# A two-layer decoder trunk on one core: the loads and squares at the start regrouped, and a new table of priorities for the order of all engines

## The chip, the cores and the metric

The kernel runs on one core of a Trainium2 chip. The metric is the time of one execution on the device, in microseconds (us); the figure for the kernel before is the median of three runs. The core has five engines that run side by side, each through its own row of instructions in a fixed order: TensorE (PE in the profile; PEld is its loading of stationary operands), VectorE (DVE), ScalarE (ACT), GpSimd (POOL) and SyncE (SP), which here only issues transfers. Sixteen DMA engines carry the transfers. An engine waits on semaphores for what another has to finish first.

## The reference

The input is x (256 tokens by 1024 features) and a condition c of 1024 values. Cut to its skeleton:

```
cs = silu(c)
for layer in range(2):
    sh1, sc1, g1, sh2, sc2, g2 = split(cs @ mod_w[layer] + mod_b[layer], 6)
    h = rms_norm(x, norm_g[layer, 0]) * (1 + sc1) + sh1
    if layer == 0:
        proj = h @ ab_w_in                       # 1024 -> 512 + 3 * 512
        y = concat(s5_mixer(proj[:512]), attention(proj[512:])) @ ab_w_out
    else:
        y = conformer_conv(h)    # GLU, causal conv of width 31, layer norm, silu, product
    x = x + g1 * y
    h = rms_norm(x, norm_g[layer, 1]) * (1 + sc2) + sh2
    x = x + g2 * conv_ffn(h)
return rms_norm(x, final_g)
```

What stands at the start of every layer, and what the change touches first, is this: the mean of the squares of x over its features, the modulation vectors from c, and then h, feature block by feature block, into the first product.

## The kernel before

Activations lie transposed: 128 features on the partitions, 256 tokens along the row, so x is eight tiles (kt = 0 to 7) of 128x256. Weights come from HBM in chunks of 512 KB (128x1024 f32). The names in the rows are buffers: `raw` and `ABT` hold weight chunks (raw_69 to raw_76 are eight of them, used over and over), `bank_61` to `bank_64` are the accumulators of the main products, `bank_65` to `bank_68` the auxiliary ones, `nt` (nt_98 to nt_101) the normalised feature tiles, `arena` the scratch space of the state-space part, `mrow` and `modv` the modulation vectors, `csv` the condition spread out as an operand, `hb` the conformer's normalised tile split in two parts for the product.

Nothing is issued as written. The functions record instructions, each with a group name (`nc.group`), and `flush` (L472), which is called after the first mixer, after the first FFN, after the conformer and at the end, hands each batch to `arrange` (L488). This is a list scheduler: it keeps a modelled clock for each engine and picks at each point the ready instruction of the highest rank. The rank is the longest path to the end plus a number from the table `BONUS` (L71) for the instruction's group. `cost` (L355) prices each instruction, a transfer by its bytes over a rate. At most eight transfers of SP and ACT are under way at once. Since every instruction is issued from one line of `flush`, all rows of the profile carry L485; the operands tell them apart.

At the start, `load` (L858) issues the small parameters (`pp`, whose first eight columns are c), x in two halves and the identity, clears a few buffers and derives `cs` and `csv`; `pump` (L602) streams weights. `start` (L1757) adds dummy products of a zero operand (groups `warm@t`, shown as `bank<-whi_81 128x512`) on PE, and the state-space preparation: `s5_poles` (66 small steps on DVE), `s5_powers` on POOL, then larger products on DVE (`arena` 128x256, 128x768 and 128x1024). `phase_a` (L1094) squares x, sums over the partitions on PE with a matrix of ones (`ones,nt`, `ones,u`), and from that makes the norm: DVE `nm`, ACT root, DVE `nm` again, DVE `dg`, and the PE product `dg,ones`, which spreads the factor over all partitions. For each kt it then runs `mods` (two halves of eight rows `raw,csv`), `select` (`sel,mrow`), `feature` (DVE `modv`, `gp`, `nt`, then ACT) and `main` (eight products `nt,raw` for kt below 4).

The conformer's layer norm, in the third batch, does the same in its middle: sums (`ones,nacc`, `ones,nt`, `negc,nt`), `nm`, `dg`, `dg,ones`, then DVE `nt`, ACT, DVE `hb`, and the next product `hb,whim`. Around it lie bundles of `raw,csv` and `ABT,csv` rows, the modulation of a later step, which need only their weights; in a bundle four chunks are used together, the rows of a chunk in a quarter of the array each.

Of the kernel before, what the change touches and what calls it, by code (L numbers as in the profile page):

```python
# [16 lines left out]
OP = mybir.AluOpType  # L17
# [262 lines left out]
class Plan:  # L280
# [74 lines left out]
    def cost(self, op):  # L355
        eng, fn, a, k, _ = op
        if fn == "dma_start":
            b = self.size(a[0]) * a[0].shape[0] * 4
            return max(0.06, b / 360e3)
# [187 lines left out]
class Emit:  # L547
# [298 lines left out]
    def modulate(self, l, j, q):  # L846
        nc = self.nc
        sh = self.modcols(l, 3 * j)
        self.h_u(0, q)
        for k in range(KT):  # L850
            if k + 1 < KT:
                self.h_u(k + 1, q)
            u, c = self.nt[k % 4], sh[:, k:k + 1]
            hi, lo = halves(self.h[:, k, :])
            nc.scalar.activation(hi, u, AF.Identity, bias=c)
            nc.vector.scalar_tensor_tensor(lo, u, c, hi.bitcast(F32), op0=OP.add, op1=OP.subtract)

    def load(self):  # L858
        nc, d = self.nc, self.d
        xv = d["x"].rearrange("(k p) t -> p k t", p=128)  # L860
        nc.sync.dma_start(self.pp[:, 0:NPAR_FIRST], d["pp"][:, 0:NPAR_FIRST])
        nc.sync.dma_start(self.x[:, 0:4], xv[:, 0:4])
        nc.sync.dma_start(self.x[:, 4:8], xv[:, 4:8])
        nc.sync.dma_start(self.ident, d["eye"][:, 0:128])
        nc.vector.memset(self.ones, 1.0 / D)
        nc.vector.memset(self.epst, EPS)
        nc.vector.memset(self.negc, -1.0 / 128)
        nc.vector.memset(self.zero2, 0.0)
        nc.sync.dma_start(self.sel, d["eye"][:, 256:260])
        nc.gpsimd.memset(self.csv, 0.0)  # L870
        nc.vector.memset(self.mrow[:, 0:512], 0.0)
        for t_ in self.AB + self.CA + [self.KD]:
            nc.gpsimd.memset(t_, 0.0)
        nc.vector.tensor_copy(self.zero, self.mrow[:, 0:512])
        self.warm(AF.Silu)
        nc.scalar.activation(self.cs, self.par("c", 0, 8), AF.Silu)
        self.warm(AF.Sqrt)
        for s in range(3):
            nc.vector.tensor_copy(self.csv[:, s, :, s], self.cs)
        nc.vector.tensor_scalar(self.gneg, self.par("norm", 0, 40), -512.0, None, op0=OP.mult)  # L880
# [213 lines left out]
    def phase_a(self):  # L1094
# [65 lines left out]
        for k in range(KT):  # L1160
# [4 lines left out]
            if k == 3:  # L1165
                v.tensor_tensor(sq[0], sq[0], sq[1], op=OP.add)
                v.tensor_tensor(sq[2], sq[2], sq[3], op=OP.add)
# [894 lines left out]
```

## Time and profile before

| | |
|---|---|
| three runs | 657.36, 657.41, 658.21 us; median 657.41 |
| profiled execution | 656.32 us |
| its span, first to last instruction | 654.5 us |
| PE busy | 641.0 us, 98% of the span |
| DVE, ACT, POOL busy | 548.3, 395.7, 52.8 us |
| mean granted clock of TensorE | 0.997 |

The profiled execution is 1.1 us below the median; 1.8 us of it lie outside the span. Its rows are read in the order of the kernel: what PE waits for, then the stretch in which a wait stands, engine by engine.

### The profile page before, as it was taken

The numbers are of one execution on the slowest core, as the hardware profiler recorded it, in microseconds if no ns is written. First come the engines' busy times: TensorE is split into PE (matmuls) and PEld (weight loads), VectorE is DVE, ScalarE is ACT, GpSimd is POOL, SyncE is SP. The second block draws the span as 40 slices with busy tenths as digits, with TensorE's granted clock in tenths as the row PEclk, the third lists the DMA queues.
The fourth block names the chain that finished last, engine by engine and source line by source line (L and its number), as shares of the span: only waits on it lengthen the run. The fifth ranks groups of instructions, "written<-read, shape, count | busy, mean of one in ns | idle before, by whom it ended". The sixth has DMA issues, their size and how long they took to land.

```text
span 654.5 us, 13232 instructions
## 1 busy us (share of the span) xinstructions
PE 641.0 (98%) x5125; PEld 564.0 (86%) x5125; DVE 548.3 (84%) x1097; ACT 395.7 (60%) x706; POOL 52.8 (8%) x101
## 2 busy tenths in 40 slices
PE   7999999999999999999999999999999999999995
PEld 6779956899999999998899987568988888888884
DVE  6899998578999999988867899569899999996642
ACT  4478444587866666654546843377596777774430
POOL 6690100000000000000000222000000000000000
PEclk9999999999999999999999999999999999999998
DMA  8996979456478899998862696595567777865001
GB/s 330 349 366 243 340 308 379 167 198 215 136 247 325 310 331 305 341 324 283 304 195 92 194 367 212 181 413 196 182 187 221 229 224 244 278 214 191 1 0 65
DMA packets 46566, 158.50 MB, mean 242 GB/s; under 512 B 5375, under 2 KB 9000, under 8 KB 46504
## 3 DMA queue, kind: packets, MB, share of 16 engines
q1 hardware_dynamic: 44936, 153.78, 67.2%
q0 software_dynamic: 1152, 3.49, 1.7%
q8 instruction: 40, 0.66, 0.4%
q10 hardware_dynamic: 416, 0.39, 0.2%
q14 instruction: 22, 0.18, 0.1%
HBM read 153.10 MB, written 1.06 MB: 236 GB/s over the span
## 4 chain that ended last, share of the span: by engine, by line
PE 94%; DVE 2%; ACT 2%; POOL 1%; issue 0%; DVEq 0%
PE bank L485 94%; POOL arena L485 1%; DVE nt L485 1%; ACT whim L485 0%; ACT h L485 0%; DVE x L485 0%; DVE whi L485 0%; ACT nt L485 0%; DVE arena L485 0%; ACT L485 0%; DVE h L485 0%; ACT cb L485 0%; DVE nm L485 0%; DVE g L485 0%; DVE mrow L485 0%
## 5 line engine op out<-in xcount | busy, mean ns | idle before, releaser
L485 PE MATMUL bank<-h,whi 128*128 128x256 f32 (+2 forms) x960 | 200.6, 303 | 0.0
L485 PEld LDWEIGHTS bank<-h,whi 128*128 128x128 f32 x960 | 151.3, 189 | 9.3 <-issue 1.8
L485 PE MATMUL bank<-h,wlo 128*128 128x256 f32 (+1 forms) x560 | 152.2, 282 | 0.0
L485 PE MATMUL bank<-h,whim 128*128 128x256 f32 (+1 forms) x664 | 150.0, 311 | 0.3 <-DVE h L485 0.3
L485 PE MATMUL bank<-h,wlom 128*128 128x256 f32 x416 | 116.6, 281 | 0.0
L485 PEld LDWEIGHTS bank<-h,whim 128*128 128x128 f32 x664 | 108.5, 189 | 8.4 <-DVE h L485 0.7
L485 PEld LDWEIGHTS bank<-h,wlo 128*128 128x128 f32 x560 | 103.2, 189 | 0.1
L485 DVE TENSOR_TENSOR wlo<-raw,whi 128x1024 fp32r<-128x1024 f32 x70 | 84.6, 1221 | 7.5 <-ACT whi L485 7.2
L485 ACT ACTIVATE whi<-raw 128x1024 fp32r<-128x1024 f32 x70 | 73.5, 1055 | 24.2 <-PE bank L485 12.0
L485 PEld LDWEIGHTS bank<-h,wlom 128*128 128x128 f32 x416 | 78.3, 188 | 0.0
L485 DVE TENSOR_TENSOR wlom<-raw,whim 128x1024 fp32r<-128x1024 f32 x57 | 69.3, 1221 | 7.4 <-ACT whim L485 7.3
L485 ACT ACTIVATE whim<-raw 128x1024 fp32r<-128x1024 f32 x57 | 59.7, 1054 | 23.5 <-PE bank L485 18.4
L485 PE MATMUL bank<-hv,whim 128*128 128x512 f32 (+1 forms) x236 | 67.7, 351 | 0.0
L485 PE MATMUL bank<-hv,whi 128*128 128x512 f32 x160 | 56.6, 394 | 0.0
L485 PE MATMUL bank<-hv,wlom 128*128 128x256 f32 x192 | 53.9, 281 | 0.0
L485 PEld LDWEIGHTS bank<-hv,whim 128*128 128x128 f32 x236 | 41.3, 188 | 6.2
L485 PE MATMUL bank<-hv,wlo 128*128 128x256 f32 x160 | 44.7, 279 | 0.0
L485 DVE SCALAR_TENSOR_TENSOR ac<-g,pp,ac 128x256 f32<-128x256 f32 x88 | 42.2, 482 | 2.2 <-ACT ac L485 0.4
L485 DVE SCALAR_TENSOR_TENSOR x<-bank,modv,x 128x256 f32<-128x256 f32 x54 | 25.6, 481 | 21.6 <-PE bank L485 20.7
L485 ACT ACTIVATE g<-bank 128x256 f32<-128x256 f32 x40 | 15.3, 382 | 39.2 <-PE bank L485 39.2
L485 PEld LDWEIGHTS bank<-hv,wlom 128*128 128x128 f32 x192 | 36.4, 189 | 0.0
L485 PEld LDWEIGHTS bank<-hv,whi 128*128 128x128 f32 x160 | 30.0, 187 | 7.1
(214 smaller groups left out, 1085.3 us busy)
## 6 DMA issues: line engine op xcount, KB each, us to landing
raw<-w_in SPq DMA_DIRECT2D x203, 512.0 KB, 5.2
ABT<-w_in SPq DMA_DIRECT2D x81, 512.0 KB, 5.0
a<-ap POOLq DMA_DIRECT2D x24, 142.0 KB, 5.6
x<-x_in SPq DMA_DIRECT2D x2, 512.0 KB, 4.6
arena<-scr SPq DMA_DIRECT2D x1, 1024.0 KB
cb<-c_in SPq DMA_DIRECT2D x2, 512.0 KB, 5.6
arena<-bc_in SPq DMA_DIRECT2D x1, 512.0 KB, 8.2
out<-x SPq DMA_DIRECT2D x2, 256.0 KB, 2.4
```

The lines of the kernel that those rows point to most:

```text
L485: getattr(getattr(self.nc, eng), fn)(*a, **k)
```

## The change

In `load`, c gets a transfer of its own (eight columns of `pp`) and goes first, on ScalarE's queue; the identity follows on the same queue. x goes in four transfers of 256 KB instead of two of 512 KB, on SP; `sel` and the rest of `pp` stay on SP. In `phase_a` the squares are taken in pairs of tiles (128x512), pairs 0 and 2 on ACT, 1 and 3 on DVE, into qT and u instead of nt and u; one addition for each pair follows on DVE, and still four sums go to PE. Each of these steps gets a group name of its own, so that the table can move it. There are 21 dummy products instead of 27. The model's transfer rate goes from 360e3 to 390e3 bytes per us. And every number of `BONUS` is new, so the order changes on all engines, most of all in the start and the first mixer.

```diff
-BONUS = {'a-evac': 702.8, 'a-gate_tail': -74.2, 'a-lead': 5, 'a-low': -1.7, ...
+BONUS = {'a-evac': 7.6, 'a-gate_tail': -3.3, 'a-h_u': -1.2, 'a-low': -0.6, ...
@@ def cost
-            return max(0.06, b / 360e3)
+            return max(0.06, b / 390e3)
@@ def load
-        nc.sync.dma_start(self.pp[:, 0:NPAR_FIRST], d["pp"][:, 0:NPAR_FIRST])
-        nc.sync.dma_start(self.x[:, 0:4], xv[:, 0:4])
-        nc.sync.dma_start(self.x[:, 4:8], xv[:, 4:8])
-        nc.sync.dma_start(self.ident, d["eye"][:, 0:128])
+        nc.group = "loadc"
+        nc.scalar.dma_start(self.pp[:, 0:8], d["pp"][:, 0:8])
+        for i in range(4):
+            nc.group = "loadx%d" % i
+            nc.sync.dma_start(self.x[:, 2 * i:2 * i + 2], xv[:, 2 * i:2 * i + 2])
+        nc.group = "loadid"
+        nc.scalar.dma_start(self.ident, d["eye"][:, 0:128])
+        nc.group = "loadsel"
+        nc.sync.dma_start(self.sel, d["eye"][:, 256:260])
+        nc.group = "loadpp"
+        nc.sync.dma_start(self.pp[:, 8:NPAR_FIRST], d["pp"][:, 8:NPAR_FIRST])
...
@@ def phase_a
-        sq = [t[:, 0:T] for t in self.nt] + [self.u[:, m].rearrange("p a b -> p (a b)") for m in range(4)]
-        for k in range(KT):
-            if k in (2, 6, 7):
-                v.tensor_tensor(sq[k], self.x[:, k, :], self.x[:, k, :], op=OP.mult)
-            else:
-                nc.scalar.activation(sq[k], self.x[:, k, :], AF.Square)
...
+        flat = self.u.rearrange("p a b c -> p a (b c)")
+        for i in range(4):
+            nc.group = "sq%d" % i
+            s, xs = (self.qT, flat)[i // 2][:, 2 * (i % 2):2 * (i % 2) + 2], self.x[:, 2 * i:2 * i + 2]
+            if i % 2:
+                v.tensor_tensor(s, xs, xs, op=OP.mult)
+            else:
+                nc.scalar.activation(s, xs, AF.Square)
+            v.tensor_tensor(s[:, 0], s[:, 0], s[:, 1], op=OP.add)
+            self.stat_mm(KT - 1 if i == 3 else 0, s[:, 0], st)
...
@@ def start
-        for i, t in enumerate([0.0] * 4 + [2.5 + WARM * i for i in range(int(11.5 / WARM))]):
+        for i, t in enumerate([0.0] * 4 + [2.5 + WARM * i for i in range(int(8.5 / WARM))]):
```

PE at the start, before, from the last of the seventeen opening dummies to the first `select` (`whi_81` rows are dummies, `ones,...` the sums of squares, `raw,csv` the modulation):

```order
L485 MATMUL bank_61<-whi_81 128x512
L485 MATMUL bank_68<-zero_109,ident 128x2
L485 MATMUL bank_68<-ones,nt_98 128x1 x2
L485 MATMUL bank_68<-ones,nt_100 128x1 x2
L485 MATMUL bank_68<-ones,u 128x1 x3
L485 MATMUL bank_65<-raw_69,csv 32x128 x8
L485 MATMUL bank_68<-ones,u 128x1
L485 MATMUL bank_65<-raw_70,csv 32x128 x8
L485 MATMUL bank_62<-whi_81 128x512
L485 MATMUL bank_63<-whi_81 128x512
L485 MATMUL bank_64<-whi_81 128x512
L485 MATMUL bank_68<-sel,mrow 128x2
```

And now, from the fifth dummy after `zero,ident` (twelve dummies stand before that row, four between) to the second half of `mods`:

```order
L485 MATMUL bank_61<-whi_81 128x512
L485 MATMUL bank_68<-ones,qT 128x1
L485 MATMUL bank_62<-whi_81 128x512
L485 MATMUL bank_68<-ones,qT 128x1 x3
L485 MATMUL bank_68<-ones,u 128x1 x2
L485 MATMUL bank_63<-whi_81 128x512
L485 MATMUL bank_64<-whi_81 128x512
L485 MATMUL bank_61<-whi_81 128x512
L485 MATMUL bank_65<-raw_69,csv 32x128 x8
L485 MATMUL bank_68<-ones,u 128x1 x2
L485 MATMUL bank_65<-raw_70,csv 32x128 x8
L485 MATMUL bank_66<-raw_71,csv 32x128 x8
```

The sums are spread out: three dummies and a half of `mods` stand ahead of the last two rows instead of the half alone ahead of the last one, and nine dummies that filled the row between `mods` and `main` are gone.

DVE at the features of kt = 2 (nt_100), before; the `arena` rows are the state-space products, 128x16x16 and 128x256 the first six, 128x16x48 the next:

```order
L485 TENSOR_TENSOR arena<-arena 128x16x16 x2
L485 TENSOR_TENSOR arena<-arena 128x256
L485 TENSOR_TENSOR arena<-arena 128x16x16 x2
L485 TENSOR_TENSOR arena<-arena 128x256
L485 TENSOR_TENSOR arena<-arena 128x16x48
L485 TENSOR_TENSOR modv_88<-bank_68,pp 128x1 x2
L485 SCALAR_TENSOR_TENSOR gp<-modv_88,gneg 128x1
L485 SCALAR_TENSOR_TENSOR nt_100<-x,gp,bank_67 128x256
```

And now:

```order
L485 TENSOR_TENSOR arena<-arena 128x16x16 x2
L485 TENSOR_TENSOR modv_88<-bank_68,pp 128x1
L485 TENSOR_TENSOR arena<-arena 128x256
L485 SCALAR_TENSOR_TENSOR gp<-modv_88,gneg 128x1
L485 TENSOR_TENSOR arena<-arena 128x16x16 x2
L485 SCALAR_TENSOR_TENSOR nt_100<-x,gp,bank_67 128x256
L485 TENSOR_TENSOR arena<-arena 128x256
L485 TENSOR_TENSOR modv_88<-bank_68,pp 128x1
L485 TENSOR_TENSOR arena<-arena 128x16x48 x2
```

The feature of kt = 2 moves ahead of the sixth small product and of the first large one.

PE in the conformer's layer norm, before, from the product that spreads the norm to the first products with `hb`:

```order
L485 MATMUL bank_65<-dg,ones 128x256
L485 MATMUL bank_64<-ABT_86,csv 32x512 x2
L485 MATMUL bank_64<-raw_73,csv 32x512
L485 MATMUL bank_64<-ABT_85,csv 32x512
L485 MATMUL bank_66<-zero_109,ident 128x2
L485 MATMUL bank_61<-hb,whim_1644 128x512
L485 MATMUL bank_61<-hb,wlom_1645 128x256
L485 MATMUL bank_62<-hb,whim_1646 128x512
L485 MATMUL bank_62<-hb,wlom_1647 128x256
L485 MATMUL bank_63<-hb,whi_79 128x512
L485 MATMUL bank_67<-raw_69,csv 32x512
L485 MATMUL bank_67<-ABT_85,csv 32x512
```

And now:

```order
L485 MATMUL bank_65<-dg,ones 128x256
L485 MATMUL bank_67<-raw_69,csv 32x512
L485 MATMUL bank_67<-ABT_85,csv 32x512
L485 MATMUL bank_67<-raw_76,csv 32x512
L485 MATMUL bank_67<-raw_72,csv 32x512
L485 MATMUL bank_64<-raw_69,csv 32x512
L485 MATMUL bank_64<-ABT_85,csv 32x512
L485 MATMUL bank_64<-raw_76,csv 32x512
L485 MATMUL bank_64<-raw_72,csv 32x512
L485 MATMUL bank_61<-hb,whim_1637 128x512
L485 MATMUL bank_61<-hb,wlom_1638 128x256
```

The two bundles of raw_69, ABT_85, raw_76 and raw_72 stood behind the first five `hb` rows and now stand ahead of them; the bundle with ABT_86 that stood there has moved ahead of `dg,ones`. The product `sg,ones`, which stood between the first two bundles of the same four buffers further up, has moved behind four of these bundles. On SP the loads that fill the four buffers anew come in the same order in both kernels, those after the change being:

```order
L485 DMA raw_69<-w_in 128x1024
L485 DMA ABT_85<-w_in 128x1024
L485 DMA raw_76<-w_in 128x1024
L485 DMA raw_72<-w_in 128x1024
L485 DMA raw_74<-w_in 128x1024
```

## Rows read from the trace of the kernel before

**Rows 1.** The page's first part: busy us, share of the span, instructions
```profile
PE 641.0 (98%) x5125; PEld 564.0 (86%) x5125; DVE 548.3 (84%) x1097; ACT 395.7 (60%) x706; POOL 52.8 (8%) x101
```

**Rows 2.** Waits of PE over the whole span: us in total, times, longest
```profile
PE bank L485 <- DVE dg L485: 1.7, 1, 1.7
PE bank L485 <- DVE hb L485: 0.8, 1, 0.8
PE bank L485 <- DVE modv L485: 0.7, 1, 0.7
```

**Rows 3.** Timeline of PE, 0 to 15 us: start, us, operation, count of records
```profile
3.55 6.52 PE L485 MATMUL bank<-whi 128*128 128x512 f32 x17 [3.55 <-DVE whi L485]
...
10.15 1.03 PE L485 MATMUL bank<-ones,nt 128*128 128x1 f32 x8
...
12.36 0.38 PE L485 MATMUL bank<-ones,u 128*128 128x1 f32 x2
12.67 0.64 PE L485 MATMUL bank<-raw,csv 128*32 128x128 f32 x16
13.24 0.97 PE L485 MATMUL bank<-whi 128*128 128x512 f32 x3
```

**Rows 4.** Stretches: PE, PEld, DVE, ACT, POOL busy (count), PEclk, DMA share, GB/s
```profile
3.55:8.60 5.05, 5.05 (x12) 3.98 (x13) 1.22 (x6) 1.03 (x3) 5.05 (x3) 1.00 0.99 344
...
10.00:20.00 10.00, 10.00 (x110) 8.34 (x110) 9.55 (x79) 5.77 (x15) 1.32 (x1) 1.00 1.03 406
...
25.40:29.00 3.60, 2.64 (x31) 2.12 (x27) 3.08 (x11) 2.19 (x7) 3.05 (x11) 1.00 0.93 345
...
40.00:50.00 10.00, 10.00 (x110) 8.34 (x109) 9.96 (x14) 7.64 (x13) 7.98 (x12) 1.00 0.96 342
```

**Rows 5.** Timeline of DVE, 9 to 28 us
```profile
9.69 0.76 DVE L485 TENSOR_TENSOR u<-x 128x256 f32<-128x256 f32 x2 [2.32 <-DMA x<-x_in]
...
12.78 0.16 DVE L485 TENSOR_SCALAR nm<-bank 128x2 f32<-128x2 f32 x1
...
15.73 0.48 DVE L485 SCALAR_TENSOR_TENSOR nt<-x,gp,bank 128x256 f32<-128x256 f32 x1
...
23.62 2.53 DVE L485 TENSOR_TENSOR arena<-arena 128x256 f32<-128x256 f32 x6 [1.91 <-POOL arena L485]
...
27.88 0.48 DVE L485 SCALAR_TENSOR_TENSOR nt<-x,gp,bank 128x256 f32<-128x256 f32 x1
```

**Rows 6.** Timeline of PE, 17 to 29 us: from `main` of kt = 0 to kt = 2
```profile
17.44 1.13 PE L485 MATMUL bank<-nt,raw 128*128 128x256 f32 x4
...
18.55 5.00 PE L485 MATMUL bank<-nt,raw 128*128 128x256 f32 x22
...
28.95 1.35 PE L485 MATMUL bank<-nt,raw 128*128 128x256 f32 x5 [0.28 <-ACT nt L485]
```

**Rows 7.** Timeline of PE in the conformer's layer norm
```profile
420.88 0.70 PE L485 MATMUL bank<-sg,ones 128*128 128x256 f32 x2
...
426.65 0.70 PE L485 MATMUL bank<-dg,ones 128*128 128x256 f32 x2
...
429.43 0.50 PE L485 MATMUL bank<-hb,whim 128*128 128x512 f32 x1 [0.77 <-DVE hb L485]
...
430.55 0.62 PE L485 MATMUL bank<-raw,csv 128*32 128x512 f32 x1
...
432.78 0.39 PE L485 MATMUL bank<-hb,wlo 128*128 128x256 f32 x1
```

**Rows 8.** Timeline of PE's weight loads, the bundle behind `hb`
```profile
430.95 0.17 PEld L485 LDWEIGHTS bank<-raw,csv 128*32 128x32 f32 x3 [0.25 <-DMA raw<-w_in]
```

**Rows 9.** SP's issues to the four buffers: timeline, then time from issue to landing
```profile
422.59 0.33 SPq L485 DMA_DIRECT2D raw<-w_in  x1
...
424.59 0.38 SPq L485 DMA_DIRECT2D raw<-w_in  x1
...
raw<-w_in SPq DMA_DIRECT2D x1, 512.0 KB, 6.3
```

More of the change, by code (lines that the diff above doesn't have):

```diff
@@ L860, in load @@
         xv = d["x"].rearrange("(k p) t -> p k t", p=128)
-        nc.sync.dma_start(self.pp[:, 0:NPAR_FIRST], d["pp"][:, 0:NPAR_FIRST])
-        nc.sync.dma_start(self.x[:, 0:4], xv[:, 0:4])
-        nc.sync.dma_start(self.x[:, 4:8], xv[:, 4:8])
-        nc.sync.dma_start(self.ident, d["eye"][:, 0:128])
+        nc.group = "loadc"
[9 more added lines that the diff above has]
+        nc.sync.dma_start(self.pp[:, 8:NPAR_FIRST], d["pp"][:, 8:NPAR_FIRST])
+        nc.group = "set"
         nc.vector.memset(self.ones, 1.0 / D)
@@ L868, in load @@
         nc.vector.memset(self.zero2, 0.0)
-        nc.sync.dma_start(self.sel, d["eye"][:, 256:260])
         nc.gpsimd.memset(self.csv, 0.0)
         nc.vector.memset(self.mrow[:, 0:512], 0.0)
-        for t_ in self.AB + self.CA + [self.KD]:
+        for i, t_ in enumerate(self.AB + self.CA + [self.KD]):
+            nc.group = "clear%d" % i
             nc.gpsimd.memset(t_, 0.0)
+        nc.group = "zero"
         nc.vector.tensor_copy(self.zero, self.mrow[:, 0:512])
+        nc.group = "cond"
         self.warm(AF.Silu)
@@ L878, in load @@
         for s in range(3):
+            nc.group = "cond%d" % s
             nc.vector.tensor_copy(self.csv[:, s, :, s], self.cs)
+        nc.group = "gneg"
         nc.vector.tensor_scalar(self.gneg, self.par("norm", 0, 40), -512.0, None, op0=OP.mult)
@@ L1760, in start @@
         self.pump(5)
+        nc.group = "loadbc"
         nc.sync.dma_start(self.BC, self.d["bc"].rearrange("p (a b c) -> p a b c", a=4, b=16))
         self.pump()
+        nc.group = "loadpp2"
         nc.sync.dma_start(self.pp[:, NPAR_FIRST:], self.d["pp"][:, NPAR_FIRST:])
+        nc.group = "loadanti"
         nc.sync.dma_start(self.anti, self.d["eye"][:, 128:256])
-        for i, t in enumerate([0.0] * 4 + [2.5 + WARM * i for i in range(int(11.5 / WARM))]):
+        for i, t in enumerate([0.0] * 4 + [2.5 + WARM * i for i in range(int(8.5 / WARM))]):
             nc.group = f"warm@{t:.2f}"
```

11 lines of the change are left out of this document (1 added, 10 removed).

## Prediction

> **What bounds the kernel now.** I read the page first: PE is busy for 641.0 of 654.5 us [rows 1], so the time is PE's row of instructions plus its few holes. The list of PE's waits [rows 2] names them: 1.7 us in the final norm, 0.8 in the conformer's layer norm (for `hb`) and 0.7 at the third feature tile (for `modv`); every other wait after the start is 0.3 or less. The first mixer, where the order changes most, has none. So a new order there can save nothing in itself; it can only hand on what the start saves, or add waits. Gains can come from three places: the start up to `main` of kt = 2, the layer norm's hole, and the final norm, whose order is the same before and after. The profiled execution took 656.32 us, 1.09 below the median of 657.41; I work out a difference and subtract it from the median.
>
> **The start.** PE runs dummies from 3.55, twelve of them in 5.05 us [rows 3, 4], 0.42 each; the three at 13.24 take 0.97, 0.32 each. [...] The sums of squares end with the row at 12.36, so that `mods` follows at 12.67 and DVE's `nm` at 12.78 [rows 3, 5].
>
> After the change I add PE's row up by durations. Twelve dummies end at 8.6. Then come the identity product (two records; eight of the similar sums take 1.03, so 0.26), five dummies (1.6), one sum row (0.26), one dummy (0.32), five sum rows (1.3), three dummies (0.97), half of `mods` (0.64) and two sum rows (0.52): 14.5. These are busy times, which overlap by about 0.07 at each change (`mods` at 12.67 takes 0.64 and the next row starts at 13.24); with some eight changes the end is 13.8 to 14.5. I take 14.0, 1.3 later than 12.67.
>
> Does x come in time for that? The second half lands at 9.68 [rows 5]. The order shows 2.10 MB on SP up to and with it; after the change 2.72 MB stand up to and with the last quarter. The extra 0.62 MB take 1.5 us at the 406 GB/s of 10 to 20 us or 1.8 at the 344 of the opening [rows 4]: 11.2 to 11.5; scaling the whole way from the first issue gives 12.2. A square of a pair (two tiles, 0.76 [rows 5]) and an addition (half that) bring the last sum to 12.4 to 13.4, before PE is there at about 13.5. So x in quarters costs nothing and gains nothing, and what hides it is the dummies and `mods`; c and the identity, earlier or not, are hidden by the twelve dummies.
>
> From `nm` to the first `nt` DVE takes 2.95 us [rows 5]; four small steps fewer stand between now, some 0.2 less. That gives `nt` at 12.78 + 1.3 + 2.75 = 16.8. From an `nt` to its `main` the third tile shows 1.07 (27.88 to 28.95 [rows 5, 6]), so `main` of kt = 0 starts at 17.9 instead of 17.44, where half a us of `mods` stood in between.
>
> From there to `main` of kt = 2 PE needs 11.51 us before, of which 0.7 and 0.28 are waits [rows 2, 6]: 10.5 of work. Of this work half a `mods` (0.64) and one `select` (0.25) now lie ahead of `main`, hidden in the hole of the norm chain; two more changes between kinds of rows cost 0.2. That leaves 9.8, and `main` of kt = 2 is reached at 27.7, if its operand is there. On DVE the third `nt` waits for five small products instead of six small and one large one. They begin when POOL releases them, at 23.62 before [rows 5]; DVE's small steps end a little later now, as the norm comes 1.3 later but ten of them (0.16 for a step as short as `nm` [rows 5], less where they overlap) were moved ahead of it, so I take 24.1. Five products of 0.42 and 0.3 for `modv` and `gp` give `nt` at 26.5, and `main` 1.07 later, 27.6. Both arms meet at 27.7, against 28.95: 1.2 gained. Since PE's row in this stretch must run without any hole for that, I take **0.9**, with 0 (PE's end at 14.5, a late x) and 1.4 as ends.
>
> **The layer norm.** At first sight two bundles now fill the 0.77 us in which PE waits for `hb`. But the four buffers of these bundles are being loaded anew. Before the change the bundle starts at 430.55, behind the first `hb` rows, and the weight load of its fourth buffer still waits 0.25 us, until 430.95, for a transfer [rows 7, 8]. That is raw_72, fourth of the four issues that begin at 422.59; it is issued at 424.59 and lands 6.3 later, at 430.9 [rows 9]. The loads can start once the first bundles have read the buffers, and these come earlier only by `sg,ones`, which takes at most 0.70 [rows 7] and has moved behind them. So raw_72 lands at 430.2 to 430.9, and PE, which gets to this bundle a little after `dg,ones` and therefore about 428.5, must wait there some 1.7 us, with the ready `hb` queued behind it. Before, all of this work (two bundles, five `hb` rows) is done at 432.78. After: 430.2 + 1.85 for the bundles (430.95 to 432.78) + 1.12 for the `hb` rows (429.43 to 430.55 [rows 7]) = 433.2 to 433.9. **Loss 0.4 to 1.1; I take 0.5**, since SP's order of the four loads is the same and nothing else holds them up. If the third load doesn't lag as it does here, where over a us passes before the fourth issue follows, raw_72 could land up to a us sooner, and 0.2 to 0.5 would be gained instead: that is the other end, a gain of 0.9 only if the wait vanished wholly.
>
> **The rest.** The mixer's PE work is the same in another order: I set it at 0, between 0 and 2. DVE is busy for 9.96 of 10 us at 40 to 50 [rows 4], so little can be caught up there. Fewer dummies save nothing by themselves, since those removed lay in holes of the norm chain. The sum: -0.9 + 0.5 = -0.4, profiled 655.9, median **657.0**.
>
> **Rivals.** *Both places gain* (faster). The start gives its 0.9 and the loads of the layer norm land in time, so that its hole of 0.8 to 0.9 goes as well: -1.8, 655.6; with 1.4 at the start, 655.1. For it: the bundles would be just the work that PE lacks there. Against it: the landing at 430.9, which would have to come at about 428.5.
>
> *The mixer takes it back* (slower). The place is DVE from 30 to 110 us: its state-space products start 0.5 later (24.1 for 23.62) while PE wants its tiles 0.9 earlier. DVE has no idle time to make that up [rows 4], so PE waits until it is back in step with DVE: 0.5 late instead of 0.9 early. With 0.5 to 1.1 from the layer norm that is +1.0 to +1.6, 658.4 to 659.0; I price it at 659.0. It decides from the point where POOL's release comes after 24. Against it: DVE is idle 1.91 us just ahead of that release [rows 5], and a large product can be put off where a feature cannot.
>
> [...]
>
> *It does not do what it says.* The squares come no sooner in PE's row, so the start stays where it was and only the layer norm's loss is left: 657.9, inside the first case's own range.
>
> **How the numbers follow.** A difference of 0.2%, 1.3 us, is about what a measurement of this kernel can tell from none. The forecast, 657.0 with its own range of 656.2 to 658.5 and the last rival in it, gets 0.46. Both places gain: 0.27, and with it all gains I have not seen. The mixer takes it back: 0.18. The clock falls: 0.09. So faster 0.27, within 0.2% 0.46, slower 0.27. The range leaves out a tenth at either side: 655.2 to 659.5.
>
> **What would show it.** The last sum row should end near 14.0 and `nm` follow; `main` of kt = 2 should start at 27.6 to 28.3 with no wait for `modv`; the state-space products on DVE should start near 24.1; the layer norm should have a wait of 1 to 2 us for a transfer in the bundle right behind `dg,ones` and none for `hb`; the list of PE's waits should hold nothing above 0.5 in the mixer; the granted clock should be 1.00 at `main` of kt = 0. I am wrong if raw_72 lands before 429, if the mixer shows waits for DVE, or if the dummies' durations show a slow stretch after 13.

## The result and the profile after

The changed kernel takes 662.96 us (median of 6 runs, 661.43 to 664.17) against 657.38 (6 runs, 656.58 to 659.21) for the kernel before: ratio 1.0081, interval [1.0067, 1.0096]. It is 5.6 us slower, where 657.0 and at most 659.5 were predicted. The profiled execution took 664.17, the slowest of the six; its span is 662.3, 7.8 more than that of before. On the chip that ran e5 to e8 below, the kernel before itself took 656.5 to 658.2 us in 6 of 25 runs and 662.9 to 666.3 in the other 19.

The page's first part (busy us, share, instructions) answers to [rows 1], and the list of PE's waits to [rows 2]:

```profile
PE 646.0 (98%) x5119; PEld 566.5 (86%) x5119; DVE 549.4 (83%) x1096; ACT 393.1 (59%) x703; POOL 48.5 (7%) x101
```

```profile
PE bank L485 <- DVE qT L485: 3.7, 1, 3.7
PE bank L485 <- DVE whi L485: 2.9, 1, 2.9
PE bank L485 <- DVE dg L485: 1.7, 1, 1.7
PE bank L485 <- DVE arena L485: 0.8, 1, 0.8
```

PE is busy 5 us longer, with six instructions fewer: the same work ran slower. And there is one large new wait, for qT, the squares of x's second pair; a small one, 0.8 us for `arena`, lies in the mixer. The wait for `whi` is the start of the first dummies, 3.55 us before and 2.87 now. The timeline of PE shows where it lies, for comparison with [rows 3] and [rows 6]:

```profile
9.15 0.28 PE L485 MATMUL bank<-ones,qT 128*128 128x1 f32 x2
13.10 1.01 PE L485 MATMUL bank<-ones,qT 128*128 128x1 f32 x4 [3.67 <-DVE qT L485]
13.97 0.99 PE L485 MATMUL bank<-ones,u 128*128 128x1 f32 x4
14.82 1.63 PE L485 MATMUL bank<-whi 128*128 128x512 f32 x3
...
17.39 1.01 PE L485 MATMUL bank<-ones,u 128*128 128x1 f32 x4
...
23.86 5.14 PE L485 MATMUL bank<-nt,raw 128*128 128x256 f32 x16
```

From 9.43 to 13.10 PE has nothing to do. Behind that hole the three dummies take 1.63 us instead of 0.97 [rows 3], and each row of four sums about 1.0 us, where e16 below has 0.50 to 0.61. The stretches (PE, PEld, DVE, ACT, POOL busy, PEclk, DMA share, GB/s) say why:

```profile
8.00:13.00 5.00, 1.43 (x9) 1.16 (x7) 4.60 (x12) 0.00 (x0) 3.45 (x2) 1.00 1.03 406
13.20:23.80 10.60, 10.60 (x101) 8.28 (x101) 5.91 (x44) 1.33 (x5) 0.00 (x0) 0.50 0.92 326
...
27.00:40.00 13.00, 13.00 (x138) 10.01 (x140) 10.04 (x24) 6.59 (x13) 11.90 (x34) 1.00 0.78 272
```

The granted clock is at half, 0.50, from 13.2 on, and back up at 1.00 from 27; before the change it is 1.00 here throughout [rows 4]. `main` of kt = 0 starts at 23.86 instead of 17.44.

Why did qT come so late? x did not: the second pair had landed at 9.11, the fourth at 11.11. DVE's timeline shows what stood in front:

```profile
8.36 0.90 DVE L485 COPY arena<-pp 128x16 f32<-128x16 f32 x1 [0.45 <-DMA pp<-pp_in]
8.44 0.84 DVE L485 TENSOR_SCALAR gneg<-pp 128x40 f32<-128x40 f32 x1
9.29 2.19 DVE L485 TENSOR_SCALAR arena<-arena 128x16 f32<-128x16 f32 x1
9.37 2.11 DVE L485 TENSOR_TENSOR arena<-pp 128x16 f32<-128x16 f32 x1
11.52 0.17 DVE L485 TENSOR_SCALAR arena<-arena 128x16 f32<-128x16 f32 x1
...
11.90 0.69 DVE L485 TENSOR_TENSOR qT<-x 128x512 f32<-128x512 f32 x1
12.50 0.17 DVE L485 SCALAR_TENSOR_TENSOR arena<-arena 128x16 f32<-128x16 f32 x1
12.62 0.42 DVE L485 TENSOR_TENSOR qT<-qT 128x256 f32<-128x256 f32 x1
```

Eight small steps stand ahead of the square `qT<-x`, seven of the state-space part and `gneg`. The first waits for its parameters, and two of them last 0.90 and 2.19 us where the same kind of step takes 0.17 at 11.52; the steps queued right behind these two, at 8.44 and 9.37, end with them. POOL's timeline has the reason: they end as its clears end, at 9.23 and 11.45.

```profile
7.42 1.81 POOL L485 MEMSET KD<- 128x2048 f32 x1
9.16 2.29 POOL L485 MEMSET CA<- 128x2560 f32 x1
```

In the kernel before these steps stood behind all squares and met the last clear only at its end.

The layer norm of the conformer answers to [rows 7] and [rows 8], PE first, then its weight loads:

```profile
436.33 1.04 PE L485 MATMUL bank<-raw,csv 128*32 128x512 f32 x2 [0.29 <-DMA raw<-w_in]
437.62 0.62 PE L485 MATMUL bank<-raw,csv 128*32 128x512 f32 x2 [0.24 <-DMA raw<-w_in]
...
439.45 0.50 PE L485 MATMUL bank<-hb,whim 128*128 128x512 f32 x1
```

```profile
436.33 0.14 PEld L485 LDWEIGHTS bank<-raw,csv 128*32 128x32 f32 x2 [1.19 <-DMA raw<-w_in]
437.62 0.11 PEld L485 LDWEIGHTS bank<-raw,csv 128*32 128x32 f32 x2 [1.15 <-DMA raw<-w_in]
```

The weight loads of two bundles wait 2.3 us for transfers (PE itself stands still for 0.5 of them), and `hb` is queued behind them.

Counted between rows that stand equally far from the last product (only `main` of kt = 0 stands 18 rows nearer to it now), the 7.8 us of the two profiled executions split so: +6.42 up to `main` of kt = 0, +0.04 in the first mixer, -0.01 from there to the conformer, +0.30 and +0.66 in the conformer's two halves, +0.09 behind it, and +0.32 between the last product and the end.

### The profile page after: what moved, and what is told of

It reads as the page before. It is cut to its first block, busy times and chain, and to the rows that moved or that the text cites. A ratio compares the mean times of both kernels' runs of the same rounds, so it can differ in the third digit from the quotient of the medians.

```text
span 662.3 us, 13210 instructions
## 1 busy us (share of the span) xinstructions
PE 646.0 (98%) x5119; PEld 566.5 (86%) x5119; DVE 549.4 (83%) x1096; ACT 393.1 (59%) x703; POOL 48.5 (7%) x101
## 3 DMA queue, kind: packets, MB, share of 16 engines
HBM read 153.10 MB, written 1.06 MB: 233 GB/s over the span
## 4 chain that ended last, share of the span: by engine, by line
PE 92%; DVE 4%; DMA 3%; SPq 0%; issue 0%; ACT 0%; DVEq 0%; ACTq 0%
PE bank L485 92%; DVE arena L485 2%; DMA raw<-w_in 1%; DMA ABT<-w_in 1%; DMA pp<-pp_in 1%; SPq L485 0%; DVE wlo L485 0%; DVE x L485 0%; DVE U L485 0%; ACT whi L485 0%; DVE qT L485 0%; DVE KD L485 0%; DVE nm L485 0%; DVE dg L485 0%; DVEq L2035 0%
## 5 line engine op out<-in xcount | busy, mean ns | idle before, releaser
L485 ACT ACTIVATE whim<-raw 128x1024 fp32r<-128x1024 f32 x57 | 59.7, 1053 | 24.5 <-PE bank L485 17.5
L485 DVE SCALAR_TENSOR_TENSOR x<-bank,modv,x 128x256 f32<-128x256 f32 x54 | 25.5, 481 | 21.5 <-PE bank L485 20.8
L485 ACT ACTIVATE whi<-ABT 128x1024 fp32r<-128x1024 f32 x27 | 28.2, 1054 | 14.6 <-DMA ABT<-w_in 8.6
L485 DVE TENSOR_TENSOR wlo<-ABT,whi 128x1024 fp32r<-128x1024 f32 x27 | 33.5, 1248 | 4.1 <-ACT whi L485 4.0
```

Of the source, the lines that this page charges most:

```text
L485: getattr(getattr(self.nc, eng), fn)(*a, **k)
```

## The experiments

All ratios are against runs of the kernel before on the same chip. The text calls a run by the first part of its name, e1 to e18, and PE's wait for qT the hole.

**The clock and the hole.** Sixteen more dummies in the hole:

```diff
+            if i == fill:                      # ahead of the second pair's sum
+                for _ in range(FILL_HOLE):     # 16
+                    <dummy product>
```

> The changed kernel with 16 more dummy products (some 0.23 us each) in PE's row just ahead of the sum of the second pair of squares, where PE idles for 3.67 us (9.43 to 13.10). The sum itself comes no sooner. Theory 'the idle hole drops the clock and the lower clock does the damage': PE stays busy, the granted clock stays at 1.00 from 10 to 30 us (0.66 in the changed kernel), main of kt = 0 starts near 19.2 instead of 23.86, and the time falls by 4 to 5 us, to about 658.5. Rival 'the late square alone, or the mixer's new order, does the damage': the same start of main within 1 us and no change of the time (663.0).

658.83 us, 1.0032 [1.0017, 1.0047] (before: 656.84). The late square is untouched, but the clock stays up:

```profile
13.20:19.70 6.50, 6.26 (x102) 4.69 (x101) 5.77 (x43) 1.30 (x4) 0.00 (x0) 1.00 1.04 405
```

```profile
19.78 3.72 PE L491 MATMUL bank<-nt,raw 128*128 128x256 f32 x16 [0.23 <-ACT nt L491]
```

`main` of kt = 0 starts at 19.78, 4.1 earlier than in the changed kernel and 2.3 later than before. So of the 6.4 us at the start of the changed kernel's profiled execution 4.1 are the clock and 2.3 the late square itself. What PE does from there to the end of the mixer takes 124.70 us for 126.99 before: the new order is 2.3 shorter there. About 0.9 of that are rows that now stand ahead of `main` of kt = 0 (half a `mods` and one `select`); 1.2 of the 2.3 fall ahead of `main` of kt = 2, 1.1 behind it.

**The order on DVE.** The second pair's square and addition ahead of the small steps:

```diff
+        late = [i for i in order if ops[i][4] == "sq1" and ops[i][0] == "vector"]
...
+            order = order[:at] + late + [i for i in order[at:] if i not in late]
```

> The changed kernel with one move on DVE: the square and the addition of the second pair of x stand ahead of the small state-space steps instead of behind the eighth of them. Theory 'these small steps, held first by the parameters' transfer (landed 8.34) and then by POOL's clears, hold the square up while x has been there since 9.11': the addition ends near 10.2 instead of 13.0, PE's hole shrinks from 3.7 to about 0.8 us, the clock stays at 1.00, main of kt = 0 starts at 17.5 to 18.5, and the time falls by 5 to 6 us, to 657 to 658. Rival 'the transfer of x is what is late': the hole stays above 3 us.

659.6 us, 1.0042 [1.0025, 1.0059]: half of the loss is left. The square now starts as x lands, and takes its 0.69 us beside a clear:

```profile
8.67 0.69 DVE L489 TENSOR_TENSOR qT<-x 128x512 f32<-128x512 f32 x1 [1.46 <-DMA x<-x_in]
```

The wait for qT is gone, but now the steps are in the way of the fourth pair, and PE waits 1.5 us for u; the clock still falls in the profiled execution (the 48 records of `raw,csv` at 14.74 take 2.32 us, for 1.52 in e1). `main` of kt = 0 starts at 19.76, not at 17.5 to 18.5: I had not asked where the stretched steps would go.

**The clears.** Two of POOL's five clears (CA and KD) on ACT, the order on DVE untouched:

```diff
+        late = [i for i in order if ops[i][4] in ("clear2", "clear4")]
...
+                    self.nc.scalar.activation(t[:, s:s + 512], zero, AF.Copy)
```

> The changed kernel with POOL's last two clears (KD and one CA, which run from 7.42 to 11.45) done by ACT as copies of a zero tile, 512 columns each, after its own two squares; DVE's row is unchanged. Theory 'DVE's small steps wait for POOL's clear in progress to end': the steps at 8.36 and 9.29, 0.90 and 2.19 us in the changed kernel, take 0.2 each, the square of the second pair starts at 9.2, its sum follows at about 10.4, the clock stays at 1.00, and main of kt = 0 starts near 17; time about 656.5 to 657.5. Rival 'they are slow for another reason (the transfer, or DVE's own queue)': they still take 0.9 and 2.2, and the time stays near 663.

657.76 us, 1.0009 [0.9993, 1.0026]. The same steps take 0.17 to 0.18 us each once no clear runs beside them:

```profile
8.68 0.18 DVE L496 COPY arena<-pp 128x16 f32<-128x16 f32 x1 [1.15 <-DMA pp<-pp_in]
...
8.89 0.17 DVE L496 TENSOR_SCALAR arena<-arena 128x16 f32<-128x16 f32 x1
...
9.47 0.68 DVE L496 TENSOR_TENSOR qT<-x 128x512 f32<-128x512 f32 x1
```

The square starts at 9.47 for 11.90 and the hole is 1.42 us long. In the profiled execution (659.96 us) the clock fell even behind that, to 0.50 from 13.0 to 19.7; the ten times lie between 656.01 and 660.83, with mean granted clocks of 0.987 to 0.997.

**The order alone, in the kernel before.** The first seven small steps go ahead of the squares of x's second half; nothing of the change is in it:

```diff
+        early = [i for i in order if ops[i][4] == "poles" and ops[i][0] == "vector" and ops[i][1] != "memset"][:7]
...
+            order = [i for i in order[:at[0]] if i not in early] + early + [i for i in order[at[0]:] if i not in early]
```

> The kernel before with one piece of order changed: on VectorE the first seven small state-space steps go ahead of the squares of x's second half. Nothing else of the change is in it. Theory: that order alone makes the loss, because a one-source step must wait while GpSimd clears; the steps then stretch over the clears up to 11.3 us, the squares come after 11.9 instead of 9.7, TensorE idles some 2 us before the sums of u, main of kt = 0 starts at 19 to 19.8 instead of 17.4, and where the clock falls after that hole up to 3 us more are lost: 658.5 to 662. Rival: the seven steps take their 0.1 us each and fit into VectorE's wait for x from 7.4 to 9.7; then the time stays at 656.5 to 657.5.

662.13 us, 1.0078 [1.006, 1.0096]: nearly the whole loss, out of seven instructions of 0.17 us. The timelines of DVE and PE, and the stretch behind:

```profile
10.38 0.98 DVE L490 COPY arena<-pp 128x16 f32<-128x16 f32 x1 [3.01 <-DMA pp<-pp_in]
11.39 0.17 DVE L490 TENSOR_SCALAR arena<-arena 128x16 f32<-128x16 f32 x1
...
11.98 0.75 DVE L490 TENSOR_TENSOR u<-x 128x256 f32<-128x256 f32 x2
```

```profile
13.12 1.30 PE L490 MATMUL bank<-ones,u 128*128 128x1 f32 x6 [1.70 <-DVE u L490]
```

```profile
13.30:20.00 6.70, 6.70 (x48) 5.31 (x49) 3.74 (x33) 2.08 (x6) 0.00 (x0) 0.50 0.97 358
```

The first step waits until the parameters land at 10.38, then until POOL's clear ends at 11.3; the squares come 2.3 us late [rows 5], PE has its hole, the clock falls, and `main` of kt = 0 starts at 22.56. In this execution PE also waits 1.06 us for the identity, ahead of its first sums, because the dummies ended sooner (5.53 us for 6.52 [rows 3]); that is not the edit's doing, and how much of the fall of the clock belongs to it is not separated. The mean granted clock is 0.990 to 0.992 in all four runs, for 0.993 to 0.997 in those of the kernel before; e9, with a wait of 1.33 us for the identity and no late square, has 0.991 to 0.997.

**The start mended.** Square first, two clears on ACT, and dummies: four ahead of the second pair's sum, two ahead of the last, four ahead of `main`:

```diff
+FILL = {"sq1": 4, "sq3": 2, "main0": 4}
...
+            if ops[i][0] == "tensor" and dummy and ops[i][4] not in seen:
...
+                for _ in range(FILL.get(ops[i][4], 0)):
+                    <dummy product>
```

> The changed kernel with all three mends of the start together: the second pair's square ahead of the small steps on DVE, POOL's last two clears on ACT, and ten dummy products in PE's row (4 ahead of the second pair's sum, 2 ahead of the last sums, 4 ahead of main of kt = 0). Theory 'the start was spoilt by the late square, POOL's clears and the clock, and the rest of the new order is neutral': the clock stays at 1.00, main of kt = 0 starts at 16.5 to 17.5 (17.44 in the kernel before), the stretch behind it is as short as with 16 dummies, and the time is 655 to 656.5, 0.5 to 1.5 us under the kernel before. Rival 'something else in the new mixer order costs': main of kt = 0 as early, but the time above 657.5.

657.65 us (656.47 to 659.03), 0.9922 [0.9891, 0.9954], on the chip where the kernel before mostly took 664; against its 657 elsewhere it is no gain. The clock stays up (the 48 records of `raw,csv` take 1.52 us, as in e1). `main` of kt = 0 came only at 19.07, and the mixer shows new waits of PE:

```profile
PE bank L500 <- ACT KD L500: 1.6, 1, 1.6
PE bank L500 <- DVE arena L500: 0.8, 1, 0.8
```

They look like the other side of the order, squares early and state-space steps late. The trace says otherwise. The first of the state-space products (`arena` 128x256) starts 4.8 us after `main` of kt = 0 here, and 5.5 after it in e1 and e16, which have no such wait. What comes late is a transfer: on ACT, KD stands behind `whi<-ABT`, the split of a weight chunk, and on DVE a step that reads this split stands ahead of the `arena` steps. Here ACT's row starts 4.2 us later than in e16, though `main` started only 1.7 later:

```profile
82.48 1.06 ACT L500 ACTIVATE whi<-ABT 128x1024 fp32r<-128x1024 f32 x1 [9.95 <-DMA ABT<-w_in]
83.57 1.22 DVE L500 TENSOR_TENSOR wlo<-ABT,whi 128x1024 fp32r<-128x1024 f32 x1 [2.48 <-ACT whi L500]
```

```profile
78.24 1.06 ACT L501 ACTIVATE whi<-ABT 128x1024 fp32r<-128x1024 f32 x1 [7.29 <-DMA ABT<-w_in]
```

In both the chunk is issued 56.3 to 56.5 us after `main` of kt = 0; it lands 7.0 us later here and 4.4 later in e16. The waits follow it in all thirteen executions with this order of the mixer: 0 us for KD and `arena` together where the load took 4.1 and 4.4 us, 0.3 to 0.4 at 4.9 to 5.0, 1.0 at 5.6 and 5.7, 1.5 at 6.1, 1.8 at 6.4, and 2.2 to 2.4 at 6.8 to 7.0. The changed kernel itself, steps first, has loads of 5.6 (its own profile) and 6.4 (e12), and e4, with the same start, 6.9.

**The layer norm.** The two bundles put back behind the first five `hb` rows, in the changed kernel; then the new numbers for the conformer's batch alone, in the kernel before:

```diff
+            order = [i for n, i in enumerate(order[:hb[4] + 1]) if n not in two] + [order[n] for n in two] + order[hb[4] + 1:]
```

```diff
+        TABLE[0] = AFTER if self.batch in (2,) else BONUS
```

> The changed kernel with the first five hb rows of the conformer's layer norm put back ahead of the two bundles that wait for new weights (the order of the loads on SP stays). Theory 'the bundles wait 2.3 us for their transfers with the ready hb behind them': the weight loads' waits for a transfer shrink from 2.3 to under 0.5, a wait of about 0.8 for hb comes back, and the time falls by about 0.9 us, to 662.1. Rival 'the loss there is something else (sg,ones moved, the later norm chain)': no change of the layer norm's length.

> The kernel before with the new table for the conformer's batch alone: the start and the mixer stay as they are, the layer norm gets the rows of the changed kernel. Theory 'the two bundles wait for their weights ahead of the ready hb': a wait of 1 to 2.5 us for a transfer in the weight loads behind dg,ones, none of 0.8 for hb, and the time +0.2 to +1.0 us, 657.1 to 657.8 against 656.8. Rival 'the order of the norm is better, and only the late start hurt it': time 0.8 us lower, 656.0.

The first gave 662.87, no gain: PE waits 2.2 us for `hb` there instead. The second gave 665.09, 1.0042 [1.0005, 1.0078] against all 25 runs of the kernel before. Its ten runs all lie above 663.8; set against the 19 longer runs of the kernel before alone, its mean is 0.9 us higher (665.19 for 664.25), with an interval of 0.0 to 1.8. That is the size of the theory, at the edge of the noise. The kernel before and this order again, with the zero operand's copy on ACT in both, so that the start is the same:

```diff
+                if fn == "tensor_copy" and a[0].tensor.name.startswith("whi") and eng == "vector":
+                    self.nc.scalar.activation(a[0], a[1], AF.Copy)
+                    continue
```

> The kernel before with one instruction moved: the copy that makes the dummies' zero operand (whi from mrow) goes from VectorE to ScalarE. Theory: the two levels of the kernel before, 7 us apart, come from this copy alone, which VectorE is let in for either between two of GpSimd's clears (1.9 us) or only behind them all (9.7 us). Then this kernel has one level, PE starts before 4 us, and the time is 656 to 657.5 wherever it runs; where the kernel before stands at 664 it is 7 us faster. Rival: the levels have another cause (the transfers, the clock); then this kernel shows them too.

> The last kernel, and the new table of numbers for the conformer's batch alone. Theory: the two bundles ahead of the ready hb wait for their transfers, as in the changed kernel; the loss is 0.4 to 1.1 us against the last kernel, with about 2.3 us of waits for raw and none for hb. Rival: the 0.7 us seen in the segments is an accident of one execution; then the two kernels agree within 0.2 us.

658.26 with the old numbers, 1.0018 [1.0003, 1.0033], and 658.27 with the new, 1.0026 [1.001, 1.0042]: no difference that these runs can tell, the means being 0.3 us apart with an interval of -1.0 to 1.6. (For the first theory of e9 nothing follows: the kernel before had one level on that chip. In e9 PE starts 0.75 us earlier, waits 1.3 us for the identity, and the clock falls for a while after it: three dummies at 13.33 take 1.63 us, for 0.97 in [rows 3].) The profile of e9 shows why a loss is hard to see. With the old order the same bundle as in [rows 8] waits 0.9 us here, not 0.25:

```profile
PEld bank L488 <- DMA raw<-w_in: 0.9, 1, 0.9
```

From the first row of these bundles to the sixth `hb` row, behind which both orders have done the same 88 products, the profiled executions took, in us: old order 13.28 (the kernel before), 13.86, 13.97, 14.01, 14.54, 14.71, 15.00, 15.26; new order 13.52, 13.78, 14.01, 14.04, 14.21, 14.24 (the changed kernel), 14.39, 14.43, 14.58, 15.03, 15.47. The means are 14.33 and 14.34, and their difference is known to about 0.6 us either way. So a loss of half a us is neither shown nor excluded.

**The rest of the table.** The changed code with the old numbers everywhere:

> The changed kernel's code (four transfers of x, squares in pairs, c and the identity on ScalarE's queue, 21 dummies) with the table of the kernel before. DVE takes all squares ahead of the small steps here, and POOL clears in the old order. Theory 'the numbers of the new table, not the loads and squares, do the damage': no hole above 1.5 us ahead of the sums, main of kt = 0 at 16.5 to 18, time 655.5 to 658. Rival 'the smaller transfers and the fewer dummies do it': a hole of 3 us or a stretch at the lower clock, and a time above 660.

676.15 us (4 runs, 669.37 to 677.16; ratio 1.02). `main` of kt = 0 starts at 17.23, but the mixer takes 137.5 us, with PE waiting 4.0 for `raw` and 3.0 for `nt`. The old numbers don't fit the new loads, so this doesn't price the table; it shows that the new code, without the new order on DVE, has no late start.

**The dummies.** The kernel before without the ten late ones:

```diff
+        warm = [i for i in order if ops[i][4].startswith("warm@")]
+        order = [i for i in order if i not in warm[17:]]
```

> The kernel before with its last ten dummy products (13.24 to 16.43) left out and nothing else moved. Theory 'a thin row of PE alone, without a late square, is enough to drop the clock': a stretch of some us at the lower clock between 13 and 25 us, main of kt = 0 up to 0.5 us later, 1 to 3 us lost in the rows up to kt = 2, time 658 to 660. Rival 'it takes a hole of 3 us': clock 1.00 all through, time 656.8.

663.78 us, 1.0015 [0.9965, 1.0065]. The granted clock falls late in the start (0.50 from 21.5 to 24.8), yet `main` of kt = 0 comes at 24.37, as in e6 on that chip (24.40) with its dummies. The median of its nine longer runs is 663.80, that of the 19 of the kernel before 664.14; its one short run took 656.01. So the clock does fall where the dummies are taken out (the mean granted clock is 0.993 to 0.994 in all ten runs), but it falls so late in the start that it costs nothing that can be seen.

**A version without the loss.** All of the mending, with the old numbers in the conformer; then with both squares early and no added dummies; then also without the three dummies ahead of the modulation:

> The changed kernel with its start mended and the conformer's batch under the old numbers: the second pair's square ahead of the state-space steps on VectorE, two of the five clears and the copy of the zero operand on ScalarE, four dummies ahead of the second pair's sum and two ahead of the last, none ahead of main, old numbers in the conformer's batch. Theory: with the hole and the late norm gone nothing of the loss is left; main of kt = 0 starts at 17 to 18.5 us, the clock stays at its upper level, and the time is 655.5 to 657, at or just below the kernel before at its lower level. Rival: the new order of the mixer or of the last FFN costs something of its own; then it stays above 658 with main of kt = 0 as early as that.

> The last mended version without its six added dummies, and with the square and addition of the fourth pair ahead of all but the first seven state-space steps on VectorE. Theory: then the start follows the sum that I had made, last sums at 13.5 to 14, main of kt = 0 at 17 to 17.7, with no hole above 1 us and no fall of the clock, and 656 to 657.5 in all. Rival: the start of the change is longer in itself; then main of kt = 0 comes after 18.3 again.

> The same without the three dummies ahead of the first half of the modulation. Theory: these dummies stand on the path now (0.97 us), so main of kt = 0 starts at 16.1 to 17 and the time is 655.5 to 657; it would then beat the kernel before if the clock stays up. Rival: without them TensorE idles between the sums, the clock falls, and 2 to 4 us are lost: 658 to 660.

657.99 us, 1.0021 [1.0005, 1.0037]; 660.52, 1.0053 [1.0036, 1.0071]; 659.41, 1.0039 [1.0018, 1.006]. `main` of kt = 0 starts at 18.85, 18.42 and 18.41. In the first and second PE waits 1.6 and 1.5 us for KD, behind loads of 7.0 and 6.8 us as in e5; in the second and third the clock falls (the first 16 records of `main` take 5.40 us in e13, for 3.72 in e16, and the granted clock is 0.50 from 14.0 to 20.5 in e14). None of the three beats the kernel before, and none shows that early squares make the mixer wait. The last version leaves the steps first, takes the two clears off POOL as in e3, and fills the 1.42 us that are left with six dummies:

> The changed kernel with two of GpSimd's clears on ScalarE, as in e3, and six dummies (1.5 to 2 us) in the hole of 1.42 us that e3 has left ahead of the second pair's sum. The steps stay ahead of the squares on VectorE, so that the state-space tiles are ready in time. Theory: without the hole the clock stays up, main of kt = 0 starts at 17 to 17.8 us, no long wait follows in the mixer, and the time is 655.3 to 657, at or a little below the kernel before. Rival: the mixer waits for its state-space tiles instead, as in e5, e11 and e13; then 657 to 658.5.

657.81 us (12 runs, 655.06 to 659.66), 1.0013 [1.0002, 1.0024] against 657.22. Its profiled execution, the fastest, reaches `main` of kt = 0 and of kt = 2 near the times that I had summed up (timeline of PE, then the stretch):

```profile
9.34 1.62 PE L499 MATMUL bank<-whi 128*128 128x512 f32 x6
10.79 0.50 PE L501 MATMUL bank<-ones,qT 128*128 128x1 f32 x4
...
13.04 0.61 PE L501 MATMUL bank<-ones,u 128*128 128x1 f32 x4
...
17.35 3.72 PE L501 MATMUL bank<-nt,raw 128*128 128x256 f32 x16 [0.23 <-ACT nt L501]
...
27.74 3.72 PE L501 MATMUL bank<-nt,raw 128*128 128x256 f32 x16
```

```profile
13.20:17.30 4.10, 3.84 (x74) 2.88 (x74) 3.30 (x29) 1.32 (x4) 0.00 (x0) 1.00 1.05 406
```

Its span is 653.3 us, 1.2 less than that of before, and its mixer takes 124.74 us. Over all its runs it doesn't beat the kernel before. Two more profiles of it ask why:

> The kernel of e16 once more, for one profile: its profiled execution took 655.06 us and eleven others 656.05 to 659.66 at about the same granted clock, so something that this profile doesn't show differs from one execution to the next. Theory: it is when transfers of weights land, as in the conformer's layer norm, where the same rows ended 13.3 to 15.3 us after their first in the kernels before; then this execution shows it there or in the loads behind it, as waits of the weight loads for raw. Rival: the start differs (when x lands, when the clock falls); then main of kt = 0 comes after 18 us or the clock is low there.

> The same a third time, with the same two readings: main of kt = 0 at 17 to 17.8 us and the difference in the conformer's batch if transfers make it; main of kt = 0 late or a low clock ahead of it if the start makes it.

656.03 and 657.52 us, `main` of kt = 0 at 17.89 and 17.50, the layer norm's stretch 14.21 and 14.43 after 14.01. Most of the difference of the slower one lies in the mixer, 126.60 us for 124.74, where PE waits 0.9 us for `raw`, 0.8 for `arena` and 0.3 for KD; e16's own execution has only 0.2, for `raw`. The waits of the slower one:

```profile
PE bank L501 <- DMA raw<-w_in: 0.9, 2, 0.7
PE bank L501 <- DVE arena L501: 0.8, 1, 0.8
PE bank L501 <- ACT KD L501: 0.3, 1, 0.3
```

So the landing of weights varies from one execution to the next, more in the mixer than in the layer norm where I had put it, and the tiles come later with it: the load ahead of KD takes 4.4 us in e16, 4.9 in e17 and 5.7 in e18, where it is also issued 0.7 later. Why one load takes 4 us and another 7 is open.

**The control.** The changed kernel unaltered, beside e9 to e11:

> The changed kernel once more, beside the others of this row. Theory: its loss stands in itself, with VectorE let in late for the second pair's square and the clock that falls after it, so it gives 662 to 664.5 again, whatever the kernel before shows here: a ratio of 1.008 to 1.010 where that stands at 657, of about 1.00 where it stands at 664. Rival: its time moves with that of the kernel before; then the ratio stays at 1.008.

662.59 us (4 runs, 661.83 to 664.77), 1.0092 [1.0068, 1.0117]; the wait for qT is 3.0 us, the clock is at half from 14.6 to 21.4 by the length of PE's rows (1.08 us for half a `mods` at 15.10, 0.64 at 21.51), and `main` of kt = 0 starts at 22.54. Its loss is its own.

## Why the prediction was wrong

**What bounds the kernel** held: PE, busy for 646.0 of 662.3 us, and its few holes.

**The start is the step that failed.** Up to `main` of kt = 2 the forecast was -0.9 us; the profiled execution, the slowest of its six, has +6.7 (35.62 for 28.95), that of e12 +3.9 (32.87).

It was not PE's sum. That gave 14.0 for the end of the last sums, 17.9 for `main` of kt = 0 and 27.7 for kt = 2; e16, which has the order of the change but neither stretched steps nor hole, has 13.65, 17.35 and 27.74. Part of that agreement is luck: PE's row starts 0.7 us earlier in e16 (2.87) than the sum assumed and holds six dummies more (1.6 us), while the sum priced its dummies too high (1.6 for five, which take 1.41). Nor was it x, which landed at 9.1 and 11.1 us where I had 11.2 to 12.2 for its end.

It was the sentence "A square of a pair ... and an addition ... bring the last sum to 12.4 to 13.4": it takes DVE to be free when x lands. I had seen that ten small steps were moved ahead of the norm, and booked them only as an advantage of the state-space part; I did not ask what they were moved ahead of. They were moved ahead of the second pair's square, with the transfer of their parameters and POOL's clears in front of them. e15 shows that moving seven such steps costs 4.9 us in the kernel before, e3 that the clears make most of it in the changed one, and e1 that 2.3 us are the delay and the rest the clock: 4.1 in the profiled execution, 2.8 in that of e12 (22.54 for e1's 19.78).

A row of before, not among those I had read, gave warning. DVE's first copy takes 1.86 us there beside POOL's clears, the same copy 0.61 us on ACT in e9:

```profile
1.63 1.86 DVE L485 CAST whi<-mrow 128x512 fp32r<-128x512 f32 x1
```

**The clock falls** had a chance (0.09) that was too small. In e8, without the ten late dummies, it falls too, to 0.50 from 21.5 to 24.8, but without a cost that can be seen. The idle time that cost came earlier, ahead of the second pair's sum. The upper end of the range, 659.5, has 2.5 us for a fall of the clock in it, a term that no run shows. The runs showed 2.8 in e12, where half speed lasts 6.8 us; in the profiled execution it lasts 13.7, through the whole norm chain, and takes 4.1 at the start and 1.4 more in the mixer. A stretch of before without a fall, 2.64 of 3.60 us busy at a clock of 1.00 [rows 4], has a hole of 0.7 at most.

**The layer norm** went as told: the weight loads of the first two bundles wait 2.3 us for transfers, and `hb` stands ready behind them. The size, +0.5, is not settled. The two profiles have +0.66, e6 has +0.9 (0.0 to 1.8), e10 against e9 +0.3 (-1.0 to 1.6), and the means of eight and eleven executions 0.0 (-0.6 to 0.6). One premise was weak: the kernel before had the earliest landing of its eight in the one execution that I had read, so that its 0.25 us of waiting [rows 8] was a low draw; the other seven have 0.8 to 2.0.

**The mixer** was set at 0 and measures +0.04, which is luck, since it is a sum: 2.3 us less of work and waits (e1, e16), of which about 0.9 only moved ahead of `main` of kt = 0, and about as much given back, 1.4 by the low clock that lasts until 26.8 (the first 16 records of `main` take 5.14 us, for 3.72 in e1) and 1.0 by waits for KD and `arena`. These waits are a sign that I had named, but not the rival that the mixer takes the start's gain back: that rival wants the state-space products to be late, and the runs show a late load of a weight chunk, with the steps first (e4, e12) as with the squares first (e5, e11, e13).

**Left open:** the 0.3 us between the last product and the end, which come with the new code (e7, with the old numbers, has them too, and e6 doesn't).

## What to carry to other kernels

When a change moves small instructions ahead of something, list what they pass on their own engine, and for each of them what it waits for: seven steps of 0.17 us, moved ahead of the squares that feed TensorE, cost 4.9 us in e15. The hole in front of the chain of short products cost the changed kernel twice, 2.3 us for the late square and 4.1 for the clock behind it, so price such a hole with the clock at 1.00 and at 0.50. And a wait for a transfer in one profile is one draw of its landing (0.25 us in the one that I had read, 0.8 to 2.0 in the other seven): before it carries a term, see it in several executions. When a wait names a tile, follow the tile's engine back; here KD was late because the row ahead of it on ScalarE waited for a weight chunk, which landed 7.0 us after its issue in e5 and 4.4 in e16.

## What the runs showed of the hardware

**In these runs one-source steps on VectorE lasted until GpSimd's clear ended, two-source steps didn't.** In the changed kernel a copy of 128x16 beside a clear took 0.90 us, a product with a scalar 2.19, and each ended with the clear (9.26 and 11.48, for 9.23 and 11.45); without one they take 0.17 to 0.18 (e3). Additions with two operands take their usual 0.42 to 0.43 us beside clears (5.45 and 7.48 in the changed kernel), squares their 0.69 (8.67 in e2). The product of two operands at 9.37, with 2.11 us, is no exception: it is queued behind the step of 2.19 and ends with it. What I had not expected is that clears issued back to back did not always let VectorE in between them. VectorE's first copy took 1.86 us in the kernel before; in e6 it waited for all the clears, the last of which ended at 11.04 us, and was done at 11.3:

```profile
1.63 9.69 DVE L489 CAST whi<-mrow 128x512 fp32r<-128x512 f32 x1
```

PE then starts at 11.4 us instead of 3.55. The 7 us between the two times of the kernel before on that chip are probably this; it was not tested, since the version with the copy on ACT met a chip on which the kernel before had only its lower time.

**The clock fell behind short holes.** It fell to 0.50 after a hole of 3.67 us (the changed kernel), after one of 1.70 with one of 1.06 shortly before (e15), in one execution after 1.42 (e3), and in e14 after three of 0.22 to 0.37 us, the first at 10.0 and the last at 13.5; in one execution of e9 three dummies took 1.63 us for 0.97 after a hole of 1.33. In e16, with none above 0.3 from 9.0 to 17.3 us, it stayed at 1.00. The length of the hole alone doesn't decide: behind one of 0.71 us in e18 and one of 0.67 in the kernel before it stayed up as well (a mean of 0.997 over all of e18, and 1.00 from 25.4 to 29.0 in the kernel before).

**The same load lands 4.1 to 7.0 us after its issue.** That is the chunk ahead of KD in the thirteen executions with the new order of the mixer; in the changed kernel itself 5.6 and 6.4.
